# Holding x stationary, two heads side by side, in the diagonal products of a chunked scan

## The chip, the core and the metric

The kernel runs on one core of one Trainium2 chip. The time is device microseconds of that core for one launch. Its engines run beside each other and wait for one another through semaphores: TensorE (PE; its weight loads are listed as PEld), VectorE (DVE), ScalarE (ACT), GpSimd (POOL) and SyncE (SP), on whose queue nearly all DMAs are issued.

## What is computed

One layer of an encoder with three groups of heads side by side, for a prompt of 256 tokens and a sample of 1024, with shared weights:

```
hn = rms_norm(x, norm_g);  proj = hn @ w_in
o_ssd = group_norm((y_forward + y_backward + d_skip * xs) * silu(z_ssd))   # a chunked scan in both directions
o_att = window_attention(q, k, v, sink) * silu(z_att)
o_mem = attention over 256 memory tokens * silu(z_mem)
return x + concat[o_ssd, o_att, o_mem] @ w_out
```

The change is in the scan. It works in chunks of L = 128 tokens; within a chunk, for each of 16 heads of 64 features, the diagonal part is

```
decay  = exp(where(tril, acs_i - acs_j, -inf))
cb     = einsum('bcign,bcjgn->bcijg', Cm, Bm)
y_diag = einsum('bcijgr,bcjgrp->bcigrp', cb[..., None] * decay, xdt)
```

so for each head a 128 x 128 matrix (token j by token i, with both directions in one matrix) times x of that head (128 tokens by 64 features).

## The kernel before

The ten token tiles of 128 (eight of the sample, two of the prompt) are cut into two groups of five. The bulk of the work is the big projections: blocks that stream one weight matrix through TensorE, with every float32 operand split into two float32r halves (`wsplit`, lines 200 to 204: ScalarE makes the high half wh, VectorE the low half wl), so that each product is three matmuls (lines 254 to 256 for token-major blocks, 512 columns streamed each; lines 289 to 291 for feature-major ones, 320 columns; lines 1199 to 1201 for blocks of a seven-product scheme at the start and the end). Raw weights come by DMA on SyncE's queue into four buffers, the halves into three.

Everything else is side work, written as generators that stop at each `yield` and stand in two lanes. Lane 0 holds the attentions (`attn`, `mem_attn`), lane 1 the scan (`ssd_up`, `ssd_down`). After each step k of a projection block, `pump` (line 155) adds that block's rates (`RATES`, line 32) to what each lane is owed and runs whole steps; so a `yield` in a generator moves what follows it later by one step of its lane, and a generator with more yields takes its lane longer. `need` (line 166) runs steps at once until a named piece is done: the fill of the output projection's operand (`refill_o`, line 1405) demands `ssd_down` of tiles 0 to 4 in this way at step 11 of one of the feature-major blocks. At step 9 of the third output block (line 1588) both lanes are run empty, and the scan's buffers are given to the last stage. The instructions of one engine run in order. The framework orders each engine's instructions ahead of time, by priority and by when it holds them ready.

`ssd_up(t)` (line 801) handles one token tile going up: it transposes x to token-major (`xsT`, line 848; PSUM tile pxs), forms the chunk's states, and builds for each quarter q of four heads the decay matrices: `rows(q)` (line 838) issues two DMAs that broadcast rows of cumulated sums into the tiles rf and mt (tag rb, three buffers), `expo(q)` and `choose(q)` turn them into exponentials (ScalarE and VectorE), `weights(q)` (line 924) multiplies by cb. `diag(g)` (line 929) then makes, for a group g of eight heads, the eight products into one PSUM tile py (128 tokens x 512): the 128 x 128 matrix is the stationary operand, 64 columns of x are streamed. VectorE multiplies x by the skip coefficients, adds the off-diagonal part and adds py (lines 936 to 939), and a DMA stores ya to yp (line 940), which `ssd_down` reads later.

All PSUM tiles of side work come from one pool of three (`psum`, line 82). `wb` (line 798) gives one of four SBUF tiles of 128 x 512. The blocks that the prediction compares with are the values of the window attention (`values`, line 670; PSUM tile po, line 675: 64 weight columns, written to PSUM partitions 0 to 63 and 64 to 127 in turn), the transposes of q (pq, line 617), of x (pxs, line 852) and of the scan's result (pr, line 995, copied by line 997 to so), and the memory attention's transposed weights (pmt, line 762; copied by line 766 to mpT, used by pmo, line 777). psc is the scores' PSUM tile, ppt and pst those of the window attention's transposed weights and of the scan's states.

Of the kernel before, what the change touches and what calls it, by code (L numbers as in the profile page):

```python
# [15 lines left out]
AF = mybir.ActivationFunctionType  # L16
# [3 lines left out]
P = 128  # L20
# [23 lines left out]
def hymba_encoder_kernel(  # L44
# [7 lines left out]
    V, A, G, T, S = nc.vector, nc.scalar, nc.gpsimd, nc.tensor, nc.sync  # L52
# [29 lines left out]
    def psum(name):  # L82
        return mix.tile([P, 512], F32, tag="mix", name=name)
# [3 lines left out]
    ident = identr.bitcast(F32)  # L87
# [35 lines left out]
    def hv(ap, n=8):  # L123
        return ap.rearrange("p (h d) -> p h d", h=n)

    def hb(ap, n, d):
        return ap.unsqueeze(2).broadcast_to([P, n, d])
# [670 lines left out]
    def wb(name, dtype=F32, shape=(P, 512)):  # L798
        return mp.tile(list(shape), dtype, tag="wb", name=name, bufs=WBB)

    def ssd_up(t):
# [33 lines left out]
        mts = {}  # L835
# [12 lines left out]
        xsT = []  # L848
# [69 lines left out]
        def choose(q):  # L918

            rf, mt = rows_[q]  # L920
            V.copy_predicated(hv(mt, 4), upper.bitcast(U32).unsqueeze(1).broadcast_to([P, 4, P]), hv(rf, 4))
            A.activation(mt, mt, AF.Exp)

        def weights(q):
            mt = rows_.pop(q)[1]
            V.tensor_mul(hv(mt, 4), hv(mt, 4), cb[:, q // 2, :].unsqueeze(1).broadcast_to([P, 4, P]))
            mts[q] = mt

        def diag(g):
            py = psum("py")  # L930
            for h in range(8):
                mt = mts[2 * g + h // 4]
                T.matmul(py[:, h * 64:h * 64 + 64], mt[:, (h % 4) * P:(h % 4 + 1) * P],  # L933
                         xsT[g][:, h * 64:h * 64 + 64], start=True, stop=True)
            sk = wb("sk") if not first else ya[g]
            V.tensor_mul(hv(sk), hv(xsT[g]), hb(dco[:, 8 * g:8 * g + 8], 8, 64))
            if not first:
                V.tensor_add(ya[g], ya[g], sk)
            V.tensor_add(ya[g], ya[g], py)
            S.dma_start(yp_d[t][:, g * 512:(g + 1) * 512], ya[g])  # L940
# [15 lines left out]
        yield  # L956
        weights(1)
        yield
        diag(0)
        choose(2)  # L960
        rows(3)
        yield
        yield
        yield
        weights(2)
        yield
# [3 lines left out]
        choose(3)  # L970
        yield
        weights(3)
        yield
        yield
        diag(1)
        yield

# [556 lines left out]
    def when_done(n, then):  # L1534
# [10 lines left out]

    run(block_tok(w_in_rows("mq"), 5, ev_raw(mq_d, 0)), RATES[0]["mq"],
        extra=when_done(1, lambda: queue(1, ssd_up, range(4))))
    queue(0, mem_attn, range(5))
    tok("z0", w_in_rows("z0"), ev_gate(0, 0))
# [15 lines left out]
    def gate(name, c, after=None):  # L1565
        for b in range(2):
            feat(name, b, ev_gateT(c, 1, 2 * b), 1, after if b else None)

    run(block_tok(w_in_rows("q"), 5, ev_raw(q_d, 5)), RATES[1]["q"], extra=when_done(2, lambda: queue(1, ssd_up, range(4, 8))))
    gate("za", 0)  # L1570
    queue(0, attn, range(5, 10))
    tok("z0", w_in_rows("z0"), ev_gate(0, 5), grp=1)
    tok("z1", w_in_rows("z1"), ev_gate(1, 5), grp=1)
    queue(1, ssd_down, range(7, -1, -1))
    queue(1, ssd_up, range(8, 10))
    queue(1, ssd_down, range(9, 7, -1))
    tok("mq", w_in_rows("mq"), ev_raw(mq_d, 5), grp=1)
# [100 lines left out]
```

## Time and profile before

| | |
|---|---|
| median of 3 runs | 1816.59 us (1814.77 to 1816.9) |
| the profiled execution | 1812.52 us, span of its instructions 1810.8 us |
| granted TensorE clock | 1.0 of full speed throughout |
| TensorE busy | 1796.0 us of matmuls, 1607.7 us of weight loads |
| VectorE, ScalarE, GpSimd busy | 1249.8, 898.1, 436.2 us |
| diagonal products (line 933) | 320 instructions in 20 blocks, first at 524.9 us, last at 1476.8 us |

All durations in the prediction are from that one profiled execution. A float32 matmul of the program shows as two matmul instructions, each with its own weight load; a transpose or a float32r matmul shows as one. In the profile an operand pair such as `py<-xs,rb` names what is written, then what is streamed and what is held.

### The profile page before, as it was taken

Reading aid. Unit: us, or ns where it says so; the run is one execution under the profiler, and the core shown is the slowest. Engines: PE = TensorE matmul, PEld = TensorE weight load, DVE = VectorE, ACT = ScalarE, POOL = GpSimd, SP = SyncE. Lnnn points to the kernel's source line nnn. Section 1 sums busy time; section 2 is a strip of 40 time slices with the busy share of each in tenths; the row PEclk is TensorE's granted clock in tenths of the full one; section 3 lists DMA queues with packets and bytes.
Section 4 is the critical chain, followed back from the end, with each engine's and each line's share of the span. In section 5 each row is a group of like instructions: output and inputs, shape, how many; then the busy total and the mean of one; then the engine's idle time right before and its main releaser. Section 6 shows DMA issues by size and latency. Waiting matters only on the chain.

```text
span 1810.8 us, 30436 instructions
## 1 busy us (share of the span) xinstructions
PE 1796.0 (99%) x10546; PEld 1607.7 (89%) x10546; DVE 1249.8 (69%) x2432; ACT 898.1 (50%) x2039; POOL 436.2 (24%) x714
## 2 busy tenths in 40 slices
PE   9999999999999999999999999999999999999999
PEld 7788999999887899999989988777888888889999
DVE  5595788886657978775755856666875654766665
ACT  6554455444355656464425635644474533543332
POOL 0105889861110000000000000001100000048775
PEclk9999999999999999999999999999999999999999
DMA  8654455447544544445436355357776564654442
GB/s 292 194 172 129 133 151 147 119 133 226 158 138 146 176 144 136 123 121 147 112 99 191 114 159 176 121 174 234 225 247 194 173 199 130 216 154 150 141 145 77
DMA packets 198891, 290.58 MB, mean 160 GB/s; under 512 B 18960, under 2 KB 80464, under 8 KB 198736
## 3 DMA queue, kind: packets, MB, share of 16 engines
q1 hardware_dynamic: 198592, 288.57, 51.7%
q8 instruction: 83, 1.36, 0.3%
q14 instruction: 72, 0.59, 0.1%
q10 hardware_dynamic: 144, 0.06, 0.0%
HBM read 231.12 MB, written 57.44 MB: 159 GB/s over the span
## 4 chain that ended last, share of the span: by engine, by line
PE 64%; ACT 1%; DMA 1%; DVE 0%; issue 0%; POOL 0%; ACTq 0%; DVEq 0%
PE acc L254 9%; PE acc L256 9%; PE acc L255 9%; PE acc L289 5%; PE acc L290 5%; PE acc L291 5%; PE acc L1201 3%; PE acc L1199 3%; PE acc L1200 3%; PE py L933 2%; PE po L675 1%; PE ppt L665 1%; PE pmo L777 1%; PE accm L1200 1%; PE accm L1201 1%; PE accm L1199 1%
## 5 line engine op out<-in xcount | busy, mean ns | idle before, releaser
L203 DVE TENSOR_TENSOR wl<-wraw,wh 128x512 fp32r<-128x512 f32 (+1 forms) x480 | 338.8, 708 | 239.4 <-ACT wh L202 235.8
L254 PE MATMUL acc<-wh,xH 128*128 128x512 f32 (+1 forms) x1248 | 482.2, 387 | 0.1
L255 PE MATMUL acc<-wl,xH 128*128 128x512 f32 (+1 forms) x1248 | 473.2, 379 | 2.4 <-DVE wl L203 2.3
L256 PE MATMUL acc<-wh,xL 128*128 128x512 f32 (+1 forms) x1248 | 472.9, 379 | 0.0
L202 ACT ACTIVATE wh<-wraw 128x512 fp32r<-128x512 f32 (+1 forms) x480 | 292.8, 614 | 353.6 <-PE acc L256 181.6
L255 PEld LDWEIGHTS acc<-wl,xH 128*128 128x128 f32 x1248 | 234.6, 188 | 46.1 <-DVE wl L203 5.0
L254 PEld LDWEIGHTS acc<-wh,xH 128*128 128x128 f32 x1248 | 234.4, 188 | 44.3 <-issue 3.5
L256 PEld LDWEIGHTS acc<-wh,xL 128*128 128x128 f32 x1248 | 234.3, 188 | 43.7 <-issue 0.9
L289 PE MATMUL acc<-xH,wh 128*128 128x320 f32 x640 | 203.4, 318 | 0.0
L291 PE MATMUL acc<-xH,wl 128*128 128x320 f32 x640 | 198.9, 311 | 0.0
L290 PE MATMUL acc<-xL,wh 128*128 128x320 f32 x640 | 198.4, 310 | 0.0
L203 DVE TENSOR_TENSOR sl<-ws,sh 128x384 fp32r<-128x384 f32 x144 | 99.6, 695 | 106.4 <-ACT sh L202 106.1
L202 ACT ACTIVATE sh<-ws 128x384 fp32r<-128x384 f32 x144 | 74.6, 523 | 175.8 <-PE acc L1200 75.5
L1171 POOL TENSOR_TENSOR ws<-wraw 128x128 f32<-128x128 f32 x144 | 87.0, 604 | 210.7 <-DMA wraw<-in_w_in_pairs_dram 86.7
L289 PEld LDWEIGHTS acc<-xH,wh 128*128 128x128 f32 x640 | 120.3, 188 | 3.9 <-issue 3.5
L290 PEld LDWEIGHTS acc<-xL,wh 128*128 128x128 f32 x640 | 120.3, 188 | 2.1 <-issue 1.7
L291 PEld LDWEIGHTS acc<-xH,wl 128*128 128x128 f32 x640 | 120.2, 188 | 0.8 <-issue 0.7
L1171 POOL TENSOR_TENSOR ws<-ws,wraw 128x128 f32<-128x128 f32 x144 | 98.4, 684 | 0.0
L1171 POOL TENSOR_TENSOR ws<-wraw,ws 128x128 f32<-128x128 f32 x144 | 93.7, 651 | 11.2
L359 DVE SCALAR_TENSOR_TENSOR c<-u,vec,c 128x638 f32<-128x638 f32 (+1 forms) x96 | 89.2, 934 | 5.4 <-ACT c L356 5.2
L1171 POOL TENSOR_TENSOR wraw<-wraw 128x128 f32<-128x128 f32 x144 | 86.9, 603 | 11.2
L120 POOL TENSOR_SCALAR qr<-qss 128x8 f32<-128x8 f32 x10 | 3.3, 330 | 355.5 <-DVE qss L599 355.3
(428 smaller groups left out, 3654.3 us busy)
## 6 DMA issues: line engine op xcount, KB each, us to landing
wraw<-in_w_in_laid_dram SPq DMA_DIRECT2D x208, 256.0 KB, 2.8
wraw<-in_w_in_pairs_dram SPq DMA_DIRECT2D x80, 256.0 KB, 2.8
wraw<-in_w_out_laid_dram SPq DMA_DIRECT2D x64, 256.0 KB, 3.0
wraw<-in_w_out_pairs_dram SPq DMA_DIRECT2D x64, 256.0 KB, 2.8
rf<-ac SPq DMA_DIRECT2D x40, 256.0 KB, 3.6
rb<-ac SPq DMA_DIRECT2D x40, 256.0 KB, 3.9
wraw<-in_w_mem_laid_dram SPq DMA_DIRECT2D x32, 256.0 KB, 4.9
xst<-in_x_sample_dram SPq DMA_DIRECT2D x20, 256.0 KB, 5.2
```

The lines of the kernel that those rows point to most:

```text
L202: a = A.activation(h, raw, AF.Copy)
L203: b = V.tensor_sub(l, raw, h.bitcast(F32))
L254: T.matmul(ps[t][:, :n], sh, h[:, :n], start=(k_ == 0), stop=False)
L255: T.matmul(ps[t][:, :n], sh, l[:, :n], start=False, stop=False)
L256: T.matmul(ps[t][:, :n], sl, h[:, :n], start=False, stop=(k_ == KT - 1))
L289: T.matmul(o, sh, cur["H", q][:, m, c], start=(k == 0), stop=False)
L290: T.matmul(o, sh, cur["L", q][:, m, c], start=False, stop=False)
L291: T.matmul(o, sl, cur["H", q][:, m, c], start=False, stop=(k == KT - 1))
L359: V.scalar_tensor_tensor(out=c[0], in0=u[:, k:k + n], scalar=cw[k], in1=c[0], op0=ALU.mult, op1=ALU.add)
L1171: G.tensor_tensor(out=o, in0=x, in1=y, op=op)
L1199: T.matmul(ps[p], h, xh, start=(k_ == 0), stop=False)
L1200: T.matmul(ps[p], h, xl, start=False, stop=False)
```

## The change

`diag(g)` is cut in two. `diag_turned(g)` makes the same eight products with the operands exchanged: 64 columns of x of one head are stationary, the 128 x 128 matrix of that head is streamed, and the result comes feature-major, 64 features x 128 tokens. Even heads go to PSUM partitions 0 to 63 and odd heads to 64 to 127, so that two heads lie side by side in the array's columns. ScalarE copies the tile to an SBUF tile yt. The new `diag(g)` transposes the four 128 x 128 pieces of yt into another PSUM tile, pyt, and goes on as before. `diag_turned(0)` stands where `diag(0)` stood and `diag(0)` two steps later, within yields that were there; for group 1 two yields and `diag_turned(1)` are put ahead of the two yields before `diag(1)`, so that `ssd_up` is two steps longer.

```diff
+        turned = {}
+
+        def diag_turned(g):
+
+            py = psum("py")
+            for j in range(4):
+                for i in range(2):
+                    h = 2 * j + i
+                    T.matmul(py[64 * i:64 * i + 64, j * P:(j + 1) * P], xsT[g][:, h * 64:h * 64 + 64],
+                             mts[2 * g + h // 4][:, (h % 4) * P:(h % 4 + 1) * P], start=True, stop=True)
+            turned[g] = wb("yt")
+            A.activation(turned[g], py, AF.Copy)
+
         def diag(g):
-            py = psum("py")
-            for h in range(8):
-                mt = mts[2 * g + h // 4]
-                T.matmul(py[:, h * 64:h * 64 + 64], mt[:, (h % 4) * P:(h % 4 + 1) * P],
-                         xsT[g][:, h * 64:h * 64 + 64], start=True, stop=True)
+            py = psum("pyt")
+            for j in range(4):
+                T.transpose(py[:, j * P:(j + 1) * P], turned[g][:, j * P:(j + 1) * P], ident)
             sk = wb("sk") if not first else ya[g]
             V.tensor_mul(hv(sk), hv(xsT[g]), hb(dco[:, 8 * g:8 * g + 8], 8, 64))
...
         weights(1)
         yield
-        diag(0)
+        diag_turned(0)
         choose(2)
         rows(3)
         yield
         yield
+        diag(0)
         yield
         weights(2)
...
         weights(3)
+        yield
+        yield
+        diag_turned(1)
         yield
         yield
         diag(1)
```

## The prediction

> **What bounds the kernel now.** I read the busy times first, then the chain that ended last, then who waited for whom on TensorE. Rows of a busy time give the time, its share of the span and the number of instructions; rows of a wait give the us in total, the times, and the longest.
>
> ```profile
> PE 1796.0 (99%) x10546; PEld 1607.7 (89%) x10546; DVE 1249.8 (69%) x2432; ACT 898.1 (50%) x2039; POOL 436.2 (24%) x714
> PE 64%; ACT 1%; DMA 1%; DVE 0%; issue 0%; POOL 0%; ACTq 0%; DVEq 0%
> L933 PE MATMUL py<-xs,rb 128*128 128x64 f32 x320 | 38.2, 272 | 0.0
> PE psc L633 <- DVE lg L635: 1.4, 1, 1.4
> ...
> PE psc L633 <- ACT qT L619: 1.1, 2, 0.7
> PE pst L859 <- ACT pT L666: 0.8, 1, 0.8
> ...
> PE ppt L665 <- DVE lg L653: 0.7, 2, 0.5
> PE pmt L762 <- DVE mpr L754: 0.2, 1, 0.2
> ```
>
> TensorE is busy 99% of the span and leads the chain; the side work of attention and scan (psc, pst, ppt, pmt) makes it wait 4.2 us in all. So the end is set by how long TensorE's own list of instructions takes, and a change is worth what it adds to or takes from that list. ScalarE at 50% and VectorE at 69% have room. The program's 160 diagonal products show as 320 instructions, two for each float32 matmul, in 20 blocks (10 token tiles, 2 groups) of 16.
>
> A busy time of pipelined matmuls is not what a block costs. I take the shift of the stream around it: from the start of the last projection matmul before the block to the start of the second one after it, less two normal steps (0.23 us at 512 columns, 0.15 at 320). The timeline of TensorE around one diagonal block (start, length, instruction):
>
> ```profile
> 1060.68 0.39 PE L256 MATMUL acc<-wh,xL 128*128 128x512 f32 x1
> 1060.91 1.89 PE L933 MATMUL py<-xs,rb 128*128 128x64 f32 x16
> 1062.61 0.48 PE L254 MATMUL acc<-wh,xH 128*128 128x512 f32 x1
> 1062.92 0.39 PE L255 MATMUL acc<-wl,xH 128*128 128x512 f32 x1
> ```
>
> 1062.92 - 1060.68 = 2.24, less 0.46: a block costs **1.78 us**, and 20 of them 35.6 us. Within it an instruction takes 1.70 / 16 = 0.106 us, though it streams only 64 columns: the 128-column weight load sets that pace.
>
> **The change, part by part.** The products keep their number, 8 per group, so 16 instructions; each now loads 64 columns of x as weights and streams 128 columns of the decay matrix, heads alternating between the array's two column halves. The kernel has one block of just this kind: the attention's values (po, line 675), 64 weight columns in alternating halves, 256 streamed columns. Its timeline, then two narrow slices within it, then the weight loads:
>
> ```profile
> 1097.69 0.39 PE L256 MATMUL acc<-wh,xL 128*128 128x512 f32 x1
> 1098.01 1.52 PE L675 MATMUL po<-pT,v_all 128*64 128x256 f32 x12
> ...
> 1099.79 0.39 PE L255 MATMUL acc<-wl,xH 128*128 128x512 f32 x1
> ...
> 1098.28 0.39 PE L675 MATMUL po<-pT,v_all 128*64 128x256 f32 x2
> ...
> 1099.14 0.39 PE L675 MATMUL po<-pT,v_all 128*64 128x256 f32 x2
> ...
> 1098.01 1.06 PEld L675 LDWEIGHTS po<-pT,v_all 128*64 128x64 f32 x12 [0.35 <-issue]
> 1099.45 0.19 PEld L254 LDWEIGHTS acc<-wh,xH 128*128 128x128 f32 x1 [0.39 <-issue]
> ```
>
> Two instructions start together at 1098.28 and two at 1099.14, with four pairs begun between: a pair each 0.86 / 4 = 0.215 us. The halves do run side by side. The block costs 2.10 - 0.46 = 1.64 us for 6 pairs, so 1.64 - 6 x 0.215 = 0.35 us on top; the weight loads stand still for 0.35 us ahead of it and 0.39 us after it, so nothing is preloaded across either border. The shorter kind, with 8 instructions, confirms it:
>
> ```profile
> 588.49 0.39 PE L256 MATMUL acc<-wh,xL 128*128 128x512 f32 x1
> 588.81 1.08 PE L675 MATMUL po<-pT,v_all 128*64 128x256 f32 x8
> ...
> 590.17 0.40 PE L255 MATMUL acc<-wl,xH 128*128 128x512 f32 x1
> ```
>
> 1.68 - 0.46 = 1.22 us, less 4 x 0.215: 0.36 us. The new block streams half as many columns, so a pair takes half of 0.215, rounded up to 0.11: 8 x 0.11 + 0.36 = **1.24 us**. No row shows such pairs this dense. From below, the pairs at the same 0.11 without the border cost: 0.88. From above, no overlap: 16 x 0.11 + 0.36 = 2.12. I take 1.24, from po, the nearest row.
>
> Added are four float32 transposes per block. The nearest row is the scan's own transposes of x:
>
> ```profile
> 1337.33 0.31 PE L291 MATMUL acc<-xH,wl 128*128 128x320 f32 x1
> 1337.48 0.60 PE L852 MATMUL pxs<-identr,xc 128*128 128x128 f32 x4
> ...
> 1338.07 0.30 PE L290 MATMUL acc<-xL,wh 128*128 128x320 f32 x1
> ```
>
> 0.74 - 0.30 = **0.44 us**, 0.11 for each. So a group costs 1.24 + 0.44 = 1.68 us in place of 1.78: -0.10 us, and 20 x -0.10 = **-2.0 us**. With 0.88 it would be 1.32 (-9.2 us), with 2.12 it would be 2.56 (+15.6 us).
>
> One row speaks against the dense pace. Transposes of the split q load and stream 128 columns each in one pass:
>
> ```profile
> 556.54 0.40 PE L256 MATMUL acc<-wh,xL 128*128 128x512 f32 x1
> 556.78 0.80 PE L617 MATMUL pq<-identr,qh 128*128 128x128 f32 x8
> 557.41 0.47 PE L254 MATMUL acc<-wh,xH 128*128 128x512 f32 x1
> ```
>
> They take 0.63 / 8 = 0.079 us each, the fastest pairs of weight load and matmul in a row that I found; the new block needs 0.055. If 0.079 is a floor for any such pair, the block is 16 x 0.079 + 0.36 = 1.62 us. If it is one weight load waiting for the one before it in the same columns, two halves halve it to 0.04 and it does not bind. I lean to the second, since po's loads and matmuls start two at a time. The Trainium skill, "TensorE: Matmul & The Clock Gate", section "Back-to-back issue gap", gives about 81 ns for each load-and-matmul pair in a sustained stream with 128 columns; by it the block is estimated at 16 x 0.081 + 0.36 = 1.66 us, a group at 2.10 and the change at +6.4 us. The trace agrees with it at pq and can't show it for two halves.
>
> The copy of the result (20 on ScalarE) is new; the copy of the memory attention's transposed weights has its shape, and the wait of the matmuls behind that copy is the nearest row for the transposes' wait:
>
> ```profile
> L766 ACT ACTIVATE mpT<-pmt 128x512 f32<-128x512 f32 x20 | 11.5, 593 | 2.4 <-PE pmt L762 2.4
> PEld pmo L777: 0.6, 2
> SPq L844 <- PE py L933: 42.1, 23, 5.0
> SPq L209 <- DVE wl L203: 316.0, 145, 8.0
> SPq L1013 <- PE pr L995: 14.6, 6, 5.2
> SPq L998 <- ACT so L997: 10.6, 13, 3.6
> ```
>
> 20 x 0.593 = 11.9 us more on ScalarE, hidden by its idle half; if that cover went, weight splits behind the copy would come 0.6 us late, with three split buffers ahead of them. The transposes are two scheduling steps behind the copy and wait for it on TensorE, with the projection matmuls queued behind. In mpT, with one or two steps between, 20 such hand-overs cost 0.6 us. I add **0.6 us**; from above, all 4.2 us of side-work waits once more; from below, nothing. The extra PSUM tile from the pool of three goes into the same bounds: each of the two tiles is held for one consumer, as py was.
>
> What moves: VectorE's two or three operations of diag and the store of yp come two steps later, and that store now stands behind the two row loads of quarter 3 on SyncE's queue. Those loads wait for py's matmuls (42.1 us) as they read the buffer that these free; the turned matmuls stand at the same place and are shorter, so that wait does not grow. Nothing in the scan waits for yp. SyncE has 316 us of waiting for free weight buffers: loads run as far ahead as buffers allow, which covers it.
>
> The two added yields make ssd_up two steps longer, 20 steps in all, with no instruction of their own. Counting the yields of every generator against the rates, the scan lane today finishes ssd_down(0) three pumps before the output's fill demands it and has 3 steps left at the final drain; after it, some 5 steps are forced at that demand and 10 are left at the drain. I cost this at nothing: projection matmuls stand ready in the meantime.
>
> Sum: -2.0 + 0.6 = -1.4 us. The profiled execution took 1812.52 us (span 1810.8 and 1.72 around it), so 1811.1 for it; it stands 4.07 us below the median of the runs, 1816.59. On that median: **1815.2 us**.
>
> **The rivals.**
> *A floor per instruction* (slower). Place: each turned block; price 20 x (1.62 + 0.44 - 1.78) = +5.6, with the waits +6.2: 1822.8 us. It decides as soon as a pair can't start in under 0.08 us. For it: pq's 0.079. Against: po's pairs start at once.
> *The halves do not overlap* (the change does not do what it says): +15.6 + 0.6: 1832.8 us. Against it: the starts in po. For it: nothing but that 128 columns are no row of the trace.
> *The border cost is not paid* (faster): -9.2 + 0.6 = -8.6: 1808.0 us. Against it, a diagonal block that follows po directly:
>
> ```profile
> 1114.46 0.39 PE L256 MATMUL acc<-wh,xL 128*128 128x512 f32 x1
> 1114.78 1.51 PE L675 MATMUL po<-pT,v_all 128*64 128x256 f32 x12
> 1116.22 2.00 PE L933 MATMUL py<-xs,rb 128*128 128x64 f32 x16
> ...
> 1118.35 0.40 PE L255 MATMUL acc<-wl,xH 128*128 128x512 f32 x1
> ```
>
> 3.89 - 0.46 = 3.43 = 1.78 + 1.65: the border is paid between side blocks too.
> *The later lane*: the forced steps bunch, and the longest waits on SyncE for the scan's last transposes and copies (5.2 and 3.6 us) reach TensorE once: -1.4 + 8.8 = +7.4: 1824.0 us. Against it: the weight loads run ahead, and the last stage, which takes these outputs in, begins a whole projection block after the drain.
>
> **How the numbers follow.** The runs of before lie within 0.12%; a difference of 0.2%, 3.6 us, is about what can be told from none. Chances: forecast 0.57 (own range 1811.6 to 1818.8), floor 0.18, no overlap 0.07, no border 0.07, lane 0.11. Faster by over 0.2%, below 1813.0: no border, and 0.11 of the forecast: 0.18. Slower, above 1820.2: floor, no overlap and 0.08 of the lane: 0.33. Within: 0.49. The range leaves out no overlap, no border and the ends of the rest: 1811.0 to 1824.5.
>
> **What would show it.** The 16 turned instructions in pairs 0.11 us apart, the block at 1.24 us by the same shift, the four transposes at 0.44, TensorE's waits on the new copy below 1 us. I am wrong if single starts 0.08 or 0.11 us apart show, if weight loads stay busy across the borders, or if new idle time lies at the drain.

## The result, and the profile after

The changed kernel takes 1816.98 us (median of 22 runs, 1813.64 to 1821.6) beside 1814.29 us (median of 22 runs, 1811.15 to 1821.25) for the kernel before: a ratio of 1.0015, with a 95% interval of 1.0008 to 1.0022. It is slower by about 2.7 us; the prediction said 1.4 us faster. That 1816.98 us is close to the forecast of 1815.2 us all the same is luck: the forecast stood on three runs of the kernel before, whose median, 1816.59 us, was 2.3 us above that of the 22. The busy line and the chain by engine, from the page of the changed kernel:

```profile
PE 1796.5 (99%) x10626; PEld 1599.8 (88%) x10626; DVE 1251.1 (69%) x2432; ACT 909.7 (50%) x2059; POOL 436.1 (24%) x714
PE 19%; DVE 1%; DMA 1%; issue 1%; POOL 0%; ACT 0%; POOLq 0%; DVEq 0%; ACTq 0%
```

TensorE issues 80 instructions more (the transposes) and ScalarE 20 (the copies). The span is 1815.0 us where it was 1810.8, yet TensorE's busy time grew by only 0.5 us: the rest is idle time. In that 0.5 us two things nearly cancel, the cheaper blocks and two stretches of 3.41 us in which TensorE ran at half clock, so that its instructions took longer (both below). The chains can't be compared by their shares: followed back from the end, the one of before breaks off at 606.38 us and this one at 1420.13 us, and TensorE has most of what either covers. What this one is good for is its path at the drain, shown further down, where it leaves TensorE for VectorE, ScalarE and DMAs. TensorE's waits in the changed kernel (us in total, times, longest), the longest of side work and one of the last stage:

```profile
PE pxs L852 <- ACT pT L666: 2.1, 1, 2.1
PE pyt L945 <- ACT yt L940: 1.7, 1, 1.7
...
PE pr L1010 <- DVE yd L1001: 1.0, 1, 1.0
PE acc L254 <- DVE yt L407: 0.8, 1, 0.8
```

With 1.3 us more for pst, psc, pmt and ppt that is 6.9 us in place of 4.2, and these are four rows that the kernel before has not got: pxs, pyt, pr, and the projection's acc behind yt of line 407 (there, yt is the last stage's tile, not the new copy). The blocks themselves, on TensorE's timeline of the changed kernel (start, length, instruction), near the place shown of before:

```profile
1047.89 0.39 PE L256 MATMUL acc<-wh,xL 128*128 128x512 f32 x1
1048.21 1.09 PE L937 MATMUL py<-rb,xs 128*64 128x128 f32 x16
...
1049.57 0.40 PE L255 MATMUL acc<-wl,xH 128*128 128x512 f32 x1
...
1052.54 0.40 PE L256 MATMUL acc<-wh,xL 128*128 128x512 f32 x1
1052.78 0.60 PE L945 MATMUL pyt<-identr,yt 128*128 128x128 f32 x4
...
1053.45 0.39 PE L255 MATMUL acc<-wl,xH 128*128 128x512 f32 x1
```

By the prediction's own shift, the turned block costs 1049.57 - 1047.89 - 0.46 = 1.22 us and the transposes 1053.45 - 1052.54 - 0.46 = 0.45 us: 1.67 us in place of 1.78, as forecast. So 20 groups gain 2 us, and some 4.7 us are lost elsewhere.

**Where they are lost.** I laid the starts of the projection blocks of the two profiles beside each other. Before any scan work begins, at 403 us, the changed kernel is already 1.82 us late, most of it by a stretch at half clock (146.69 to 150.10 us) behind a wait for a weight split that both kernels have, 1.97 us long here and 1.70 us before, where the clock stayed at 1.00. The change has no part in that, so I count from there. At the start of the block at 1190 us it is 5.4 us ahead, at the start of the first output block 3.5 us ahead, and at the end of the span 2.4 us behind. A lead in the middle is partly work not done yet (the first experiment separates this); the losses fall in three places.

*Tile 7's second hand-over.* TensorE, ScalarE, VectorE and SyncE's queue in the changed kernel, with the idle time ahead of an instruction and what ended it in brackets:

```profile
1197.03 1.09 PE L937 MATMUL py<-rb,xs 128*64 128x128 f32 x16
...
1198.86 0.39 PE L254 MATMUL acc<-wh,xH 128*128 128x512 f32 x1
1200.99 0.76 PE L945 MATMUL pyt<-identr,yt 128*128 128x128 f32 x4 [1.74 <-ACT yt L940]
1201.40 0.77 PE L255 MATMUL acc<-wl,xH 128*128 128x512 f32 x1
1201.97 0.63 PE L256 MATMUL acc<-wh,xL 128*128 128x512 f32 x1
1202.40 0.63 PE L254 MATMUL acc<-wh,xH 128*128 128x512 f32 x1
```

```profile
1198.72 0.63 ACT L1051 ACTIVATE zd<-yd 128x512 f32<-128x512 f32 x1 [4.58 <-issue]
...
1200.35 0.59 ACT L940 ACTIVATE yt<-py 128x512 f32<-128x512 f32 x1
```

```profile
1197.95 0.69 DVE L1050 TENSOR_TENSOR yd<-yd,zd 128x512 f32<-128x512 f32 x1 [3.56 <-DMA yd<-yp]
```

```profile
1191.41 0.32 SPq L951 DMA_DIRECT2D yp<-ya  x1
...
1195.24 0.32 SPq L1028 DMA_DIRECT2D yd<-yp  x1
```

Read from the bottom: the first half's partial result goes out at 1191.41 and `ssd_down` asks for it back at 1195.24; VectorE stands 3.56 us for that load; ScalarE's square (line 1051) waits for VectorE, and the copy of the new products, done at about 1198.1, stands behind the square in ScalarE's queue until 1200.35. The transposes then stop TensorE for 1.74 us. The projection matmuls after it start 0.43 us apart where 0.23 is normal. Two stretches of that time (length, then the busy time of TensorE, its loads, VectorE, ScalarE, GpSimd, then the granted clock) give the reason:

```profile
1198.00:1201.41 3.41, 1.67 (x13) 1.09 (x9) 2.02 (x4) 2.21 (x5) 0.00 (x0) 1.00 0.28 69
1201.41:1204.82 3.41, 3.41 (x11) 2.73 (x9) 1.30 (x2) 0.00 (x0) 0.00 (x0) 0.50 0.92 296
```

The granted clock fell to one half for 3.41 us. Eight steps from 1201.40 to 1204.90 took 3.50 us in place of 1.84, so the slow stretch cost 1.7 us more.

*The fill.* At the start of the first output block the transposes of x (pxs) wait 2.05 us on ScalarE, which stood in turn for the scan's output that the fill had just forced out:

```profile
1343.22 0.83 ACT L196 ACTIVATE xH<-chd,vec 128x640 fp32r<-128x640 f32 x1 [2.23 <-DMA chd<-oT]
```

*The drain.* The chain of the changed kernel from the place where both lanes are run empty to TensorE's last wait (start, length, what):

```profile
1538.47 0.50 DVE yd L1001
1539.01 0.67 PE pr L1010 x4
1539.71 0.44 ACT so L1012
...
1540.36 3.83 DMA oT<-so
1544.21 3.02 DMA rb__17399<-oT
...
1556.79 4.37 DMA yt<-in_x_sample_dram
1561.25 0.70 DVE yt L407
1562.00 0.50 PE acc L254
```

The forced scan steps run to the scan's last transposes (pr), which wait for VectorE; their output is stored at 1540.36, and the last stage loads it back at 1544.21, VectorE works on what is loaded, and in the chain behind that work stands the load of x that the last stage's eviction (line 407) adds; the matmuls wait for the PSUM tile that this eviction frees. SyncE's queue in the kernel before has the same events earlier:

```profile
1531.79 0.52 SPq L998 DMA_DIRECT2D oT<-so  x1
...
1534.49 0.33 SPq L1074 DMA_DIRECT2D rb__17259<-oT  x1
...
1548.38 0.33 SPq L406 DMA_DIRECT2D yt<-in_x_sample_dram  x1
```

This store, the last but one of the scan's output, comes 8.6 us later than before (1540.36, 1531.79) and the load of x 8.4 us later (1556.79, 1548.38), though the block that contains the drain began only 0.23 us later.

### The profile page after: what moved, and what is told of

Read it like the earlier page. It is cut to its first block, busy times and chain, and to the rows that moved or that the text cites. A ratio compares the mean times of both kernels' runs of the same rounds, so it can differ in the third digit from the quotient of the medians.

```text
span 1815.0 us, 30630 instructions
## 1 busy us (share of the span) xinstructions
PE 1796.5 (99%) x10626; PEld 1599.8 (88%) x10626; DVE 1251.1 (69%) x2432; ACT 909.7 (50%) x2059; POOL 436.1 (24%) x714
## 3 DMA queue, kind: packets, MB, share of 16 engines
q8 instruction: 83, 1.36, 0.3%
```

## The experiments

Theory: the two added steps make the scan lane later, so that more of it is forced at the fill and at the drain, and TensorE waits there (the prediction's rival *the later lane*). First rival: the hand-over itself, copy and transposes, costs it. Each kernel is compared with the kernel before on its own chip.

**1. The steps alone** (`steps_alone`): the kernel before, its old diagonal block, with two empty yields.

```diff
         weights(3)
         yield
         yield
+        yield
+        yield
         diag(1)
```

> The kernel before with two empty yields added ahead of the second diagonal block of each tile, nothing else. Later lane: slower than before by what the change lost beside its blocks, +4 to +5 us (ratio 1.0025), with idle time of TensorE around the drain and in the block behind it as in the changed kernel. Rival, the hand-over: no difference, within 1 us, since no copy and no transpose is added.

Measured 1816.05 us (12 runs) against 1813.16: 1.0012 [1.0002, 1.0023]. The waits of TensorE in it:

```profile
PE pxs L852 <- ACT pT L666: 1.9, 1, 1.9
...
PE acc L254 <- DVE yt L407: 1.2, 2, 1.0
PE pr L997 <- DVE yd L988: 1.0, 1, 1.0
```

Two yields with no instruction behind them bring three of the four new waits, in the same places. From the first output block to the end, TensorE's idle time is 4.9 us here and 4.95 us in the changed kernel, beside 1.06 us before: the added 3.9 us are the steps'. That the hand-over alone made the kernel slower falls. This kernel too is 3.6 us "ahead" at the block at 1190 us, with no block made cheaper: that much of the 5.4 us was side work put off, the rest is the blocks' gain. The size was less than expected, 2.9 us by the medians. The profile shows why: from 403 us on, the 3.9 us stand against 2.6 us of idle time that are gone ahead of the first output block (0.94 in place of 3.52 us), and a stretch at half clock (1343.89 to 1347.30 us) behind the fill's wait adds 1.7; together 3.0 us, by which it is behind at the end.

**2. The change without the added steps** (`same_steps`): the changed kernel, two of its yields taken out.

```diff
         weights(3)
         yield
-        yield
         diag_turned(1)
         yield
-        yield
         diag(1)
```

> The changed kernel with its two added yields taken out: the turned products of group 1 stand one step behind the weights and the transposes one step behind them, so that the scan's generator is as long as before. Theory of the later lane: the blocks' -2 us stays, the forced steps at the final drain go back from 10 to 3 and the idle time of TensorE after them goes: about 2 us faster than before (ratio 0.999), no idle time of TensorE over 0.2 us in the block after the drain. Rival, the hand-over (TensorE waits for the new copy, ScalarE and PSUM are more crowded): as slow as the change or slower, +2.7 us or more against before, since each hand-over has one step less; waits on the copy in the waits of TensorE above 2 us.

Measured 1813.30 us (12 runs) against 1813.16: 0.9994 [0.9984, 1.0004]. The loss is gone; whether the blocks' 2 us come out whole can't be told, since the interval holds 0.999 as well as 1. The rival's 2.7 us or more fall, though its sign, a wait on the copy above 2 us, is there. The profile, which is that of the slowest of the 12 runs, has no wait for pxs and pr, 0.6 us for acc behind yt of line 407 is left, and TensorE is idle 1.85 us after the first output block's start instead of 4.95; in place of that, the wait for the copy moved:

```profile
PE ppt L665 <- DVE lg L653: 3.2, 3, 1.9
...
PE pyt L945 <- ACT yt L940: 2.2, 1, 2.2
```

```profile
1194.44 0.60 ACT L304 ACTIVATE zs<-acc 128x512 f32<-128x512 f32 x1 [2.66 <-DMA z<-zs]
...
1195.46 0.59 ACT L940 ACTIVATE yt<-py 128x512 f32<-128x512 f32 x1
```

Again the copy stands in ScalarE's queue behind an instruction that waits for a DMA, here a gate's eviction that waits for a buffer being stored.

**3. The change with a faster lane in the output blocks** (`after_rate`): the steps stay; the rate of lane 1 makes up for them before the drain.

```diff
-          ... 'o': (1.95, 1.9)})
+          ... 'o': (1.95, 2.2)})
```

> The changed kernel with the scan lane's rate in the token-major output blocks raised from 1.9 to 2.2 steps a pump, so that the lane is empty before the final drain (0 steps forced instead of 10). Later lane: the 3.5 us of idle time that the change has in the third and fourth output block go, so about 1 us faster than before; what the forced steps cost at the fill of the output operand stays. Rival, the hand-over: stays at +2.7 us against before.

Measured 1812.23 us (12 runs) against 1813.16: 0.9990 [0.9980, 1.0000]. The profile is again that of the slowest run. The rows for pr and for acc behind yt are gone; what remains is at the fill and at the hand-over, which the rate of later blocks can't reach:

```profile
PE pxs L852 <- ACT pT L666: 2.6, 1, 2.6
PE pyt L945 <- ACT yt L940: 2.0, 1, 2.0
```

From the start of the second output block to the end TensorE is idle 0.1 us, and 2.9 in the change. So the loss at the drain came from steps left over, and not from the new instructions.

**4. The same rate in the kernel before** (`before_rate`), to see whether that rate is a gain of its own. The edit is that of 3, on the old kernel.

> The kernel before with the scan lane's rate in the token-major output blocks at 2.2 instead of 1.9, the control for the changed kernel at 2.2, which was 0.1% faster than before. Theory that the rate only takes back what the added steps cost: no difference, within 1 us, since before has 3 steps left at the drain and no idle time of TensorE behind it. Rival, the rate is a gain of its own: about 0.1 to 0.2% faster as well.

Measured 1812.31 us (11 runs) against 1813.09: 0.9996 [0.9985, 1.0008]; no difference that can be told.

**5. The halves one after the other** (`halves_apart`): the changed kernel with the two loops exchanged, so that four heads go to one column half and then four to the other.

```diff
-            for j in range(4):
-                for i in range(2):
+            for i in range(2):
+                for j in range(4):
```

> The changed kernel with the two loops of the turned products exchanged: four heads into the lower column half, then four into the upper, so that neighbours in TensorE's list share a half. If the overlap of the two halves makes the block short, as predicted: 16 x 0.11 + 0.36 = 2.12 us for a block instead of 1.24, so 20 x 0.88 = +17.6 us on the change, +20 us against before (ratio 1.011). If the block is short for another reason (64-column weight loads alone): no difference to the change.

Measured 1823.43 us (4 runs) against 1813.16: 1.0052 [1.0036, 1.0068]. TensorE's timeline, then its weight loads:

```profile
1051.11 0.39 PE L256 MATMUL acc<-wh,xL 128*128 128x512 f32 x1
1051.42 1.58 PE L937 MATMUL py<-rb,xs 128*64 128x128 f32 x16
...
1053.27 0.39 PE L255 MATMUL acc<-wl,xH 128*128 128x512 f32 x1
```

```profile
1051.42 1.34 PEld L937 LDWEIGHTS py<-rb,xs 128*64 128x64 f32 x16 [0.35 <-issue]
```

The block costs 2.16 - 0.46 = 1.70 us, 0.48 us more than with the heads in turn; 20 of them give 9.6 us, and this kernel is 7.6 us above the changed one by their distances from the kernel before. It is 10.3 us above the kernel before, half of what was expected. The halves do run side by side in the change. But the exchange of the loops did not take the overlap away, so my price without it, 2.12 us, was not put to the test: at three moments of the block two instructions are in flight, then four, then two.

```profile
1051.69 0.38 PE L937 MATMUL py<-rb,xs 128*64 128x128 f32 x2
...
1051.91 0.44 PE L937 MATMUL py<-rb,xs 128*64 128x128 f32 x4
...
1052.41 0.38 PE L937 MATMUL py<-rb,xs 128*64 128x128 f32 x2
```

The starts in the trace form two rows of eight, in each of which the steps after the first are 0.109 us. By the order of the loops the second row is the upper half; it begins 0.49 us after the first row, beside its last three instructions, and the block is longer by about that. So within one half the pace is the 0.11 us of the price. In the turned block, with halves in turn, 16 matmuls start within 1.09 - 0.27 = 0.82 us, 0.055 us apart. Why the upper half begins before the lower has ended, the trace does not show. The Trainium skill, "TensorE: Matmul & The Clock Gate", section "Back-to-back issue gap", has about 81 ns for a load-and-matmul pair with 128 columns; neither the 0.109 us within one half nor the 0.055 us of two halves in turn agrees with it, and the measurement decides.

**6. The copy on VectorE** (`vector_copy`): is it ScalarE's queue that makes the copy late?

```diff
-            A.activation(turned[g], py, AF.Copy)
+            V.tensor_copy(turned[g], py)
```

> The changed kernel as it is, with the added yields, and the copy on VectorE. If the one long wait on the copy (1.7 us and the half clock after it, about 3 us) comes from ScalarE's queue alone, it goes, and the kernel comes to about before (ratio 1.000); the forced steps at the fill and at the drain stay, with their idle time. If that wait comes from the load of the scan's partial result, on which VectorE's queue waits as well, it stays: +2 to +3 us.

Measured 1817.57 us (10 runs) against 1813.09: 1.0021 [1.0012, 1.0030]: no gain. VectorE in it:

```profile
1196.86 0.69 DVE L1050 TENSOR_TENSOR yd<-yd,zd 128x512 f32<-128x512 f32 x1 [3.19 <-DMA yd<-yp]
1198.91 0.69 DVE L203 TENSOR_TENSOR wl<-wraw,wh 128x512 fp32r<-128x512 f32 x1 [1.36 <-ACT wh L202]
1199.52 0.68 DVE L940 COPY yt<-py 128x512 f32<-128x512 f32 x1
```

TensorE waits 1.6 us for this copy. The load of yp holds VectorE directly, for 3.19 us; ScalarE's square and the wh of a weight split queued behind it come late by that, VectorE's wl waits 1.36 us for this wh, and the copy stands behind wl. So on either engine the copy is queued behind what the load has made late. This profile also has a wait of 1.9 us for another load (cc, read by the matmul of pyb) that the change's profile has not got, so the two differ in more than the copy.

**7. Both: no added steps, copy on VectorE** (`same_steps_vector`): the edits of 2 and 6.

> The changed kernel without the added yields, and the copy of the turned result on VectorE instead of ScalarE. With the copy on ScalarE one of its 20 copies, that of the eighth tile's second group, stood behind a gate eviction that waited for a DMA; TensorE waited 2.2 us for it and then ran 3 us at half its clock. Theory: that one wait goes with ScalarE's queue, so about 2 us faster than before (ratio 0.999) and 3 us less in the block of the memory queries than with the copy on ScalarE. Rival: the wait comes back on VectorE, which is busier (69% against 50%): no gain over the copy on ScalarE.

Measured 1810.71 us (11 runs) against 1813.09: 0.9994 [0.9984, 1.0005]. The longest wait for the copy is 0.7 us here and was 2.2 in experiment 2, but ppt waits 4.1 us on VectorE in place of 3.2, and the ratio is the same. Which engine copies can't be told from these runs.

**8. and 9. All three: no added steps, copy on VectorE, the faster lane** (`all_three`, and again on another chip as `all_three_again`): the edits of 2, 6 and 3.

> The turned products without the added yields, the copy on VectorE, and the rate of 2.2 in the output blocks: all that stood against the blocks' gain taken out. Theory of block prices: 20 x -0.10 = -2.0 us and no new waits, so 0.9985 to 0.999 of before, the fastest of the kernels. Rival: every shift of the side work makes its own waits somewhere, so within 1 us of before.

> The fastest kernel once more, unchanged, beside the one with the copy on ScalarE: 0.9973 of before within its interval of 0.9962 to 0.9984 if that time was no accident; 0.999 or more if it was.

Measured 1808.23 us (7 runs) against 1813.09, 0.9973 [0.9962, 0.9984], and then 1810.97 us (12 runs) against 1812.39, 0.9986 [0.9976, 0.9996]. The second ratio lies between what was expected of no accident and of one; the two intervals overlap, and both are below 1.

**10. No added steps and the faster lane, copy on ScalarE as in the change** (`same_steps_rate`): the edits of 2 and 3.

> The turned products without the added yields and with the rate of 2.2 in the output blocks, the copy left on ScalarE: it tells what VectorE's copy is worth beside the other two. If the long wait for the eighth tile's second copy is what ScalarE's queue costs: 2 to 3 us slower than with the copy on VectorE, so 0.9985 to 0.999 of before. If the place of the copy does not matter: 0.997 as with the copy on VectorE.

Measured 1809.72 us (12 runs) against 1812.39: 0.9989 [0.9981, 0.9998]. In its profile the only wait for the copy is 0.2 us, and TensorE is idle 0.89 us after the first output block's start, beside 1.06 before the change. So the turned products, set in so that the scan lane gets no longer and is not left over at the drain, are 0.1 to 0.2% faster than the kernel before, about the 2 us that the blocks promised, though the rate may have a share in it (experiment 4 leaves 0.9985 to 1.0008 for the rate alone); the place of the copy makes no difference that can be told (0.9989 and 0.9986, on one chip).

## Why the prediction was wrong

- **The blocks** (-2.0 us): right. 1.22 and 0.45 us where 1.24 and 0.44 stood. The pace of the pairs, 0.11 us for two, and the 0.36 us at the border came out of po's blocks rightly, though po streams twice as many columns. The rival *a floor per instruction* fell with it, since instructions start 0.055 us apart. My reason against it, that the 0.079 us is the pace of pairs in the same columns, is not shown: within one half it is 0.109 us (experiment 5). *The border cost is not paid* fell too: the loads stand still for 0.35 us ahead of the turned block as well.
- **The added steps**: this is the step that failed. "I cost this at nothing: projection matmuls stand ready in the meantime." They stand ready, but in TensorE's queue behind the forced side work, which waits. I had counted the steps (some 5 forced at the fill, 10 left at the drain; no trace shows the count), had named new idle time at the drain as a sign of being wrong, and even had the mechanism, as the rival *the later lane* with a chance of 0.11; against it I set that the weight loads run ahead and the last stage begins later. Neither is what waits: it is pxs behind ScalarE's split of the forced output, pr behind VectorE, and the evictions of line 407 behind the last stage's late work on VectorE. Shown by experiments 1, 2 and 3. Its size was over-stated: I priced it at 8.8 us, and from the first output block on TensorE idles 3.9 us longer.
- **"Nothing in the scan waits for yp"**: wrong. `ssd_down` of the same tile loads it back as soon as it is stored, and VectorE and ScalarE stood 3.56 and 4.58 us around that load; the copy was queued behind them. The kernel before shows the same way round: its store of that half lands at 1181.71 us and the load starts at 1181.72, but VectorE uses it only at 1191.73, without a wait.
- **The waits on the copy** (+0.6 us): mis-sized. At 19 of the 20 places TensorE shows no idle time, at one 1.74 us, and the slow stretch after it costs 1.7 us more: 3.4 us in one place. From mpT I took a sum over 20 like hand-overs; one bad place decides, and the upper bound, "all 4.2 us of side-work waits once more", held it.
- **The clock**: the sum had no term for it. The mean granted clock of the 22 runs of the changed kernel is 0.9985; over the 29, 29 and 23 runs of the kernel before in the experiments it is 0.9996, 0.9997 and 0.9997. What is missing to 1, taken as time lost, is 2.8 us against 0.5 to 0.8, so I estimate that about 2 of the 2.7 us are TensorE at half clock behind its waits. It goes with the added steps: the other kernels that have them (experiments 1, 3, 5 and 6) lie at 0.9990 or below, and all without them at 0.9994 or above. The size is rough: each run's clock is given to three places only, and of the runs of the kernel before in the result section only the profiled one has a clock beside it.
- **What the parts make**: -2.0 for the blocks, +3.9 of idle time from the first output block on, +1.7 for the slow stretch, and -0.5 for idle time that is gone between 403 us and that block (3.0 in place of 3.5 us, the hand-over's 1.74 included) give +3.1; the profiles differ by 2.4 from that point and the runs by 2.7.

What stays open is what the long hand-over by itself costs in a mean of runs. Experiments 2 and 10 are the same program up to the output blocks, and its wait is 2.2 us in the one profile and 0.2 in the other: it depends on the run. Moving the copy (6 and 7) gave no difference beyond the intervals.

## What to carry to other kernels

A yield in a lane of side work is not free because it holds no instruction: count how many steps it leaves over at each place where the lane is forced to finish, and look at what the last of these steps feed. Matmuls that stand ready do not cover a wait of an instruction that is ahead of them in the same queue. Where a product gets a copy and a second pass through TensorE, look up at every such place what the copying engine has queued ahead, above all what waits there for a DMA. And price a wait of about 2 us with the stretch at half clock that it may bring: 1.7 us here, as much as the wait again.

## What the runs showed of the hardware

- *A wait below 2 us can halve TensorE's clock; where it falls decides.* The slow stretches within the traces are 3.41 us long, and in one trace they begin whole multiples of 3.41 us apart (at 146.69 and 1201.41 us in the changed kernel, 309 lengths). I cut each of the 12 traces into windows of that length, in step with its slow stretches (one of which is at the end of every trace), from 8 us after the start to 4 us before the end. In ten windows TensorE is idle for 1.74 us or more, and each of them is followed by a stretch at half clock. In all others it is idle for 1.59 us or less, and none is. In the changed kernel the 1.74 us of the hand-over lie in one window (1198.00 to 1201.41 us, shown above). The same hand-over's 2.03 us in experiment 3 were parted into 1.15 and 0.88 us by a border, and the clock stayed at 1.00:

```profile
1198.42:1201.83 3.41, 2.26 (x22) 1.52 (x20) 0.80 (x2) 1.38 (x4) 0.00 (x0) 1.00 0.37 128
1201.83:1205.25 3.42, 2.54 (x13) 2.19 (x14) 2.57 (x4) 0.83 (x2) 0.00 (x0) 1.00 0.83 213
1205.25:1208.66 3.41, 3.41 (x20) 2.91 (x19) 2.45 (x6) 0.63 (x1) 0.00 (x0) 1.00 0.76 251
```

  The Trainium skill, "TensorE: Matmul & The Clock Gate", section "What's actually happening", lets the clock fall after an idle window of about 3.4 us. The slow stretch has that length here, but a window idle for about half of it was enough; the measurement decides.
- *Two column halves run side by side, each at 0.109 us for a pair of load and matmul, so that in turn the pairs start 0.055 us apart* (the changed kernel and experiment 5), for 64 float32 weight columns and 128 streamed. The block has 0.35 us on top, 1.22 us in all.
